# Queueing two weight splits behind the recombination, and the convolution behind them, in a decoder layer's up-projection

## The chip, the core and the metric

One core of a Trainium2 chip runs the whole program. The metric is the device time of one launch in microseconds (us): the median of 3 runs of the kernel before is 1353.44 us, lowest 1352.97, highest 1354.55.

## The reference

One decoder layer on 1024 positions of width 1024, all in float32: RMSNorm, two attention mixers side by side, a gated merge and a residual, then RMSNorm and a gated MLP, whose input side is the part that matters here:

```python
u = xn @ w_up                                # (1024,1024) @ (1024, 5632)
c = conv_b
for j in range(3):
    c = c + upad[:, j:j + S] * conv_w[j]     # causal, per channel
gate, val = jnp.split(c, 2, axis=-1)
x = x + (jax.nn.silu(gate) * val) @ w_down   # (1024,2816) @ (2816,1024)
```

## The kernel before, in words

**Arithmetic.** TensorE multiplies in a rounded 32-bit format. To keep float32 precision, every operand is split into a high part (a cast on ScalarE, ACT) and a low part, the source minus the high part (a subtraction on VectorE, DVE); a product is three matmuls: high·high, high·low, low·high.

**The up-projection** (`hidden`, lines 883 to 963) takes the 44 blocks of 128 output columns as 22 pairs j = 0..21: block j is the gate, block j + 22 the value. Each pair uses a seven-product scheme (Strassen-Winograd) instead of eight products. Its steps, with the names that the text uses:

- *Loading and sums* (`sum_pair`, L93 to L104). Two transfers from the SP queue bring the raw blocks: `raw` (L93, A11 and A12) and `rv` (L95, A21 and A22). GpSimd (POOL) makes the four sums in four operations of 128x512: L98 and L102 give S1 and S2, L103 and L104 give S3 and S4. The buffers of `rv` and of the sums are two deep, so the transfer of a later `rv` waits until the low part of A22 has been taken, and L103 waits until the low part of S3 and S4 of the pair before has been taken.
- *Splitting* (`split_pair`, L120 and L121): for each of (A11, A12), (S1, S2), (S3, S4) and (A22) a cast on ACT and a subtraction on DVE. The text calls the four DVE subtractions **low11** (`wl<-raw`, 128x1024), **low12** and **low34** (`sl<-sf`, 128x1024 each) and **low22** (`wl<-rv`, 128x512).
- *Products* P1, P2, P5, P6, P7, P3, P4 in this order, 12 matmuls of 128x128 by 128x512 each into a PSUM bank of its own (in the last pair P4 stands ahead of P3). P1 multiplies A11, P4 multiplies A22. In P4 the third matmul is the first that reads low22. A product may begin when the bank that it takes has been read: P5 of a pair takes the bank that L423 of the pair before reads.
- *Recombination* (`recombine`, L422 to L429): one copy on ACT and seven additions on DVE, 128x512, which read the banks and write the two halves `us`; L428 completes the first half, L429 (the block c21) the second.
- *Convolution and gate* (`conv`, `glu`). For each half: POOL scales by the norm factor (L1014), ACT starts the convolution (L1019), DVE adds two taps (L1020, L1021, both `c<-us,vecs,c`). Then ACT takes the SiLU (L1006), DVE multiplies gate and value (L1007), and SP stores the product (L1008). The text calls the DVE steps tap1 and tap2 of the first and second half.

While the products of pair j + 1 run on TensorE, the other engines recombine and convolve pair j, and prepare pairs j + 1 to j + 3. A scheduler sets the order of instructions on each engine by priorities; `issue_after` adds that everything issued under it stands behind the named instruction on its engine. The last pair has its convolution deferred into the down-projection, and in the last two rounds the hidden blocks 0 to 2 are split as well (L793).

Of the kernel before, what the change touches and what calls it, by code (L numbers as in the profile page):

```python
# [13 lines left out]
ALU = mybir.AluOpType  # L14
# [29 lines left out]
class Trunk:  # L44
    def __init__(self, tc, ins, out):
        self.tc, self.nc = tc, tc.nc
        (self.xT, self.w_in, self.w_br, self.w_mix, self.w_up, self.w_dn,
         self.vecs_d, self.bias_d) = ins
        self.out = out
        self.uid = 0  # L50
        self.stores = []
        self.uw = self.w22 = self.behind = None
        self.pin = False
        self.hs, self.defer, self.late = {}, [], []

    def name(self, s):
# [50 lines left out]
    def split_pair(self, g, v, sa, sb, skip=0, end=4):  # L107

        nc = self.nc
        ops = {}  # L110
        for pool, h, l, src, names in ((self.wp, "wh", "wl", g, ("A11", "A12")), (self.uw, "sh", "sl", sa, ("S1", "S2")),
                                       (self.uw, "sh", "sl", sb, ("S3", "S4")), (self.w22 or self.wp, "wh", "wl", v[:, 1:2], ("A22",)))[skip:end]:
            n = len(names)
            hi = self.tl(pool, [P, n, 4, P], h, F32R)
            lo = self.tl(pool, [P, n, 4, P], l, F32R)
            with ExitStack() as queue:
                if self.pin and ops:
                    for i in done:
                        queue.enter_context(self.tc.issue_after(i.ins))
                i = nc.scalar.copy(hi, src)  # L120
                j = nc.vector.tensor_tensor(lo, src, hi.bitcast(F32), ALU.subtract)  # L121
            if not ops:
                done = i, j
            for i, name in enumerate(names):
                ops[name] = hi[:, i], lo[:, i]
        self.pin = False
        return ops

    def load_raw(self, src, nk):
# [286 lines left out]
    def recombine(self, ps, us, tp, o):  # L416

        nc = self.nc
        c11, c12, c21, c22 = (us[w][:, o + hf * H2:o + (hf + 1) * H2] for w in range(2) for hf in range(2))
        s1, u3 = (self.tl(tp, [P, H2], n, bufs=1) for n in ("s1", "u3"))  # L420
        tt = nc.vector.tensor_tensor
        nc.scalar.copy(s1, ps["P1"])  # L422
        tt(c11, ps["P2"], s1, ALU.add)  # L423
        tt(s1, ps["P6"], s1, ALU.add)
        tt(u3, ps["P7"], s1, ALU.add)
        tt(c22, ps["P5"], u3, ALU.add)
        tt(s1, ps["P5"], s1, ALU.add)
        tt(c12, ps["P3"], s1, ALU.add)  # L428
        tt(c21, u3, ps["P4"], ALU.subtract)  # L429

    def keep(self, m, u, to):

# [450 lines left out]
    def hidden(self, pair):  # L883
        nc, tc = self.nc, self.tc
        with ExitStack() as ctx:
            e = ctx.enter_context
            psF = e(tc.tile_pool(name="psF", bufs=8, space=PSUM, reuse_waits="tile"))
            self.psT = psF
            xc2 = e(tc.tile_pool(name="xc2", bufs=1, side="right", reuse_waits="tile"))
            self.uw = e(tc.tile_pool(name="uw", bufs=3, side="right", reuse_waits="tile"))  # L890
            prods = (("P1", "A11", "B11"), ("P2", "A12", "B21"), ("P5", "S1", "T1"), ("P7", "S3", "T3"),
                     ("P3", "S4", "B22"), ("P6", "S2", "T2"), ("P4", "A22", "T4"))
            with tc.high_priority(400):
                w0 = self.split_pair(*pair)
            ready = {}
            for j in range(NF):
                w, ps = ready.pop(j) if j else (w0, {})
                if j == 0:

                    for name, a, b in prods[:5]:  # L900
                        ps[name] = self.tl(psF, [P, H2], "t")
                        self.product(ps[name], w[a], b, range(3), last=False)
                    for k in range(4):
                        hi, lo = self.split(*(xc2.tile([P, T], F32R, name=f"T42_{k}{p}") for p in "hl"), self.t42[k])
                        self.B["T4", k], self.B["T2", k] = ((hi[:, c], lo[:, c]) for c in (slice(0, H2), slice(H2, T)))
                        if k == HOLD:
                            self.behind, self.pin = self.lo, True
                    self.tctx.close()
                    tp = e(tc.tile_pool(name="tp", bufs=2, side="right", reuse_waits="tile"))
                    self.w22 = e(tc.tile_pool(name="w22", bufs=1, side="right", reuse_waits="tile"))  # L910
                    w22 = self.w22
                    ssq = self.tl(psF, [P, H2], "t")
                    for n, (name, a, b) in enumerate(prods[:5]):
                        self.product(ps[name], w[a], b, (3,), first=False)
                        if n == 4:
                            self.col_sums(ssq, [self.rstd], NB, 0)
                            with tc.high_priority(400):
                                rs = self.rstd_cols(ssq, 8, D)
                if j == NF - 1:

                    with tc.high_priority(50):
                        for k, r in enumerate(raw):
                            for hf in range(2):
                                h = self.tl(self.uw, [P, 2, H2], ("sh", "sl", "rv", "rv", "sh", "sl")[2 * k + hf], F32R, **({"bufs": 2} if k == 1 else {}))
                                self.hs[hf, k] = self.split(h[:, 0], h[:, 1], r[:, hf * H2:(hf + 1) * H2])
                        lo = self.lo
                for name, a, b in (prods[i] for i in ((0, 1, 2, 5, 3, 6, 4) if j == NF - 1 else (0, 1, 2, 5, 3, 4, 6) if j else range(7))):
                    if name not in ps:
                        ps[name] = self.tl(psF, [P, H2], "t")
                        self.product(ps[name], w[a], b, low_last=name == "P1")  # L930
                us = [self.tl(tp, [P, T + 2], "us", bufs=3) for _ in range(2)]
                if j == NF - 1:
                    self.defer.pop(0)(lo)
                    w22.tile([P, 104], F32, name="pad_w22")
                    self.xctx2.close()
                    self.uw = self.w22 = None
                    self.open_down()
                    self.deep = True
                    with tc.high_priority(100):
                        self.ahead(2)  # L940
                self.recombine(ps, us, tp, 2)
                if j < NF - 1:

                    w, ps = ready[j + 1] = self.next_w(), {}
                    if j == NF - 2:
                        raw = [self.tl(self.sfp[0], [P, T], "t42", bufs=1)] + [self.tl(self.sfp[0], [P, T], "sf") for _ in range(2)]
                        for k, r in enumerate(raw):
                            nc.sync.dma_start(r, self.hd[k])
                    for name, a, b in prods[:2 if j == 0 else 0]:
                        ps[name] = self.tl(psF, [P, H2], "t")  # L950
                        self.product(ps[name], w[a], b, low_last=name == "P1")
                if j == 0:
                    for hf in range(2):
                        sp = self.tl(psF, [P, H2], "t")
                        self.spread(sp, rs, hf * 4)
                        nc.scalar.copy(self.rstd[:, hf * H2:(hf + 1) * H2], sp)

                for w in range(2):
                    f = lambda after=None, j=j, w=w, us=us: self.glu(j, w, us[w], tp, after)
                    if j + w < NF - 1:  # L960
                        f()
                    else:
                        self.defer.append(f)

# [295 lines left out]
```

## Time and profile before

| | |
|---|---|
| median of 3 runs | 1353.44 us |
| profiled execution | 1352.23 us, of which the span on the core is 1350.4 us |
| granted clock of TensorE | 0.997 |
| busy: TensorE / DVE / ACT / POOL | 99% / 75% / 45% / 35% |
| pair 1's P1 begins / pair 21's P1 begins | 701.79 us / 1088.12 us |

In the timeline a row gives the start in us from the start of the span, the duration in us, the engine, the line, the operation, what it writes and reads, and in brackets the idle time ahead of it with what ended it. A matmul's duration is its way through the array; the next starts some 0.23 us after it, so the distance of starts tells the pace. DVE's rows overlap by about 0.08 us in the same way.

### The profile page before, as it was taken

Reading aid. Unit: us, or ns where it says so; the run is one execution under the profiler, and the core shown is the slowest. Engines: PE = TensorE matmul, PEld = TensorE weight load, DVE = VectorE, ACT = ScalarE, POOL = GpSimd, SP = SyncE. Lnnn points to the kernel's source line nnn. Section 1 sums busy time; section 2 is a strip of 40 time slices with the busy share of each in tenths; the row PEclk is TensorE's granted clock in tenths of the full one; section 3 lists DMA queues with packets and bytes.
Section 4 is the critical chain, followed back from the end, with each engine's and each line's share of the span. In section 5 each row is a group of like instructions: output and inputs, shape, how many; then the busy total and the mean of one; then the engine's idle time right before and its main releaser. Section 6 shows DMA issues by size and latency. Waiting matters only on the chain.

```text
span 1350.4 us, 17209 instructions
## 1 busy us (share of the span) xinstructions
PE 1332.3 (99%) x6304; PEld 1103.7 (82%) x6304; DVE 1009.0 (75%) x1457; ACT 603.3 (45%) x943; POOL 477.7 (35%) x349
## 2 busy tenths in 40 slices
PE   8999999999999999999999999999999999999997
PEld 6888888888887778888888888888888878888887
DVE  8847775288899876465679888888888988886454
ACT  8432232277667665334444334433443344333343
POOL 0436652010102124641455554555556520231011
PEclk9999999999999999999999999999999999999998
DMA  7423443966554236334422222222222239652342
GB/s 256 149 107 151 142 154 140 257 170 186 156 134 132 84 113 230 112 126 135 164 94 83 80 92 78 78 78 86 86 79 75 75 136 333 200 180 70 94 138 81
DMA packets 62468, 179.49 MB, mean 133 GB/s; under 512 B 6832, under 2 KB 15152, under 8 KB 62384
## 3 DMA queue, kind: packets, MB, share of 16 engines
q1 hardware_dynamic: 50928, 160.98, 36.8%
q10 hardware_dynamic: 11456, 17.41, 3.5%
q8 instruction: 50, 0.82, 0.3%
q14 instruction: 34, 0.28, 0.1%
HBM read 129.61 MB, written 48.76 MB: 132 GB/s over the span
## 4 chain that ended last, share of the span: by engine, by line
PE 64%; DVE 13%; issue 8%; POOL 7%; ACT 5%; DMA 2%; POOLq 0%; ACTq 0%; DVEq 0%; SPq 0%
PE t L879 6%; PE t L881 6%; PE t L880 6%; POOL us L1014 4%; PE y L1045 3%; PE d L1045 3%; PE g L176 3%; PE g L177 3%; PE g L178 3%; DVE wl L121 3%; PE sc L595 3%; PE sc L178 2%; PE sc L177 2%; PE sc L176 2%; PE d L1072 2%
## 5 line engine op out<-in xcount | busy, mean ns | idle before, releaser
L1019 ACT ACTIVATE c<-us,vecs 128x1024 f32<-128x1024 f32 x44 | 54.8, 1247 | 163.4 <-POOL us L1014 161.4
L1014 POOL TENSOR_TENSOR us<-us,rstd 128x1024 f32<-128x1024 f32 x42 | 100.3, 2405 | 52.0 <-DVE wl L143 34.6
L120 ACT CAST sh<-sf 128x1024 fp32r<-128x1024 f32 x62 | 65.0, 1050 | 113.8 <-POOL sf L102 68.6
L141 ACT CAST wh<-raw 128x1024 fp32r<-128x1024 f32 (+2 forms) x60 | 60.7, 1012 | 107.0 <-PE sc L177 30.5
L1020 DVE SCALAR_TENSOR_TENSOR c<-us,vecs,c 128x1024 f32<-128x1024 f32 x44 | 64.6, 1470 | 53.4 <-ACT c L1019 53.4
L143 DVE TENSOR_TENSOR wl<-raw,wh 128x1024 fp32r<-128x1024 f32 (+2 forms) x60 | 78.5, 1309 | 31.3 <-ACT wh L141 19.7
L98 POOL TENSOR_TENSOR sf<-rv 128x512 f32<-128x512 f32 x30 | 42.3, 1410 | 163.4 <-DVE sl L121 56.5
L121 DVE TENSOR_TENSOR sl<-sf,sh 128x1024 fp32r<-128x1024 f32 x62 | 86.1, 1391 | 11.5 <-ACT sh L120 11.4
L176 PE MATMUL g<-xh,wh 128*128 128x512 f32 x176 | 70.6, 401 | 0.1
L178 PE MATMUL g<-xh,wl 128*128 128x512 f32 x176 | 70.3, 400 | 0.0
L177 PE MATMUL g<-xl,wh 128*128 128x512 f32 x176 | 70.3, 399 | 0.0
L193 POOL TENSOR_TENSOR rs<-ms,mhalf 128x8 f32<-128x8 f32 (+2 forms) x9 | 14.5, 1606 | 157.3 <-DVE ms L191 146.7
L121 DVE TENSOR_TENSOR wl<-raw,wh 128x1024 fp32r<-128x1024 f32 (+1 forms) x35 | 61.2, 1748 | 3.7 <-ACT wh L120 3.6
L103 POOL TENSOR_TENSOR sf<-raw,rv 128x512 f32<-128x512 f32 x30 | 41.6, 1388 | 58.9 <-DVE sl L121 58.9
L599 DVE CUSTOM_DVE_ANT_0 L<-sc,bias 128x128 f32<-128x128 f32 (+7 forms) x64 | 47.7, 752 | 17.0 <-PE sc L595 13.8
L578 POOL MEMSET aT<- 128x128 f32 x32 | 6.1, 204 | 151.6 <-PE t L624 97.8
L102 POOL TENSOR_TENSOR sf<-sf,raw 128x512 f32<-128x512 f32 x31 | 58.5, 1886 | 1.6
L600 ACT ACTIVATE L<-L,sm 128x128 f32<-128x128 f32 (+7 forms) x64 | 49.6, 778 | 20.0 <-DVE sm L599 17.3
L1021 DVE SCALAR_TENSOR_TENSOR c<-us,vecs,c 128x1024 f32<-128x1024 f32 x44 | 57.2, 1302 | 0.6
L753 POOL TENSOR_TENSOR gr<-gr,rstd 128x1024 f32<-128x1024 f32 x16 | 40.4, 2531 | 40.0 <-DMA gr<-gd 39.9
L595 PE MATMUL sc<-u,u 128*128 128x512 f32 (+2 forms) x192 | 49.8, 358 | 0.0
L178 PE MATMUL sc<-mh,wl 128*128 128x512 f32 x126 | 49.1, 390 | 0.1
(479 smaller groups left out, 4323.9 us busy)
## 6 DMA issues: line engine op xcount, KB each, us to landing
u<-qd SPq DMA_DIRECT2D x72, 256.0 KB, 6.4
raw<-in_w_down SPq DMA_DIRECT2D x27, 512.0 KB, 3.7
raw<-in_w_in SPq DMA_DIRECT2D x25, 512.0 KB, 4.1
hr<-hd SPq DMA_DIRECT2D x50, 256.0 KB, 5.5
raw<-in_w_up SPq DMA_DIRECT2D x23, 512.0 KB, 3.5
hd<-c SPq DMA_DIRECT2D x22, 512.0 KB, 2.6
rv<-in_w_up SPq DMA_DIRECT2D x21, 512.0 KB, 3.5
gr<-gd SPq DMA_DIRECT2D x16, 512.0 KB, 3.6
```

The source lines that it names most:

```text
L120: i = nc.scalar.copy(hi, src)
L121: j = nc.vector.tensor_tensor(lo, src, hi.bitcast(F32), ALU.subtract)
L143: self.lo = (eng or nc.vector).tensor_tensor(wl, raw, wh.bitcast(F32), ALU.subtract)
L176: nc.tensor.matmul(ps, wh[:, kc + o, :], ah, start=first and n == 0, stop=False)
L177: nc.tensor.matmul(ps, wh[:, kc + o, :], al, start=False, stop=False)
L178: nc.tensor.matmul(ps, wl[:, kc + o, :], ah, start=False, stop=last and n == len(kcs) - 1)
L595: nc.tensor.matmul(sc[:, lo + n0:lo + n1], qs, k[c][part][:, n0:n1], start=part == 0, stop=part == 1)
L879: nc.tensor.matmul(ps, ah[:, k, :], bh, start=first and n == 0, stop=False, skip_group_check=skip)
L880: nc.tensor.matmul(ps, ah[:, k, :], bl, start=False, stop=False, skip_group_check=skip)
L881: nc.tensor.matmul(ps, al[:, k, :], bh, start=False, stop=last and n == len(ks) - 1, skip_group_check=skip)
L1014: i = (nc.vector if m % NF == 0 else nc.gpsimd).tensor_tensor(us[:, 2:], us[:, 2:], self.rstd, ALU.mult)
L1045: nc.tensor.matmul(ps, v[:, n, :], x, start=n == i == 0, stop=n == len(js) - 1 and i == 2)
```

## The change

In `hidden`, from pair 1 on, `next_w` (which splits the weights of pair j + 2) runs with `self.after` set to the last addition of the recombination (c21): the cast and the subtraction for A11 and A12 of pair j + 2 are issued after it. The cast and the subtraction of A22 of pair j + 1 and of A11, A12 of pair j + 2 are noted as `made`, and the convolutions of pair j are issued after these. Nothing is added to the work and nothing is taken from it.

```diff
@@ split_pair
+                if self.after is not None and names[0] == "A11":
+                    queue.enter_context(self.tc.issue_after(self.after.ins))
                 i = nc.scalar.copy(hi, src)
                 j = nc.vector.tensor_tensor(lo, src, hi.bitcast(F32), ALU.subtract)
             if not ops:
                 done = i, j
+            if names[0] in ("A11", "A22"):
+                ops["made", names[0]] = i, j
@@ recombine
-        tt(c21, u3, ps["P4"], ALU.subtract)
+        return tt(c21, u3, ps["P4"], ALU.subtract)
@@ hidden
-                self.recombine(ps, us, tp, 2)
+                c21 = self.recombine(ps, us, tp, 2)
+                made = []
                 if j < NF - 1:
+                    self.after = c21 if j else None
                     w, ps = ready[j + 1] = self.next_w(), {}
+                    self.after = None
+                    if j:
+                        made = [x[y] for x, y in ((w, ("made", "A22")), (self.wq[-1], ("made", "A11"))) if y in x]
@@ hidden, the convolutions
-                        f()
+                        with ExitStack() as queue:
+                            for i in made:
+                                for x in i:
+                                    queue.enter_context(tc.issue_after(x.ins))
+                            f()
```

The lines of the changed kernel stand 2 to 13 further down: the split is L122 and L123, the recombination L426 to L433, L1027, L1032, L1033, L1034 are the scaling and the three steps of the convolution, L1019 and L1020 SiLU and gate, L1021 the store.

The DVE queue in the steady part of the up-projection, before, from the last two additions of one pair (`us_1212`, `us_1213`) to the middle of the next pair's (`us_1237`); `wl_1202` is low22 of the pair after `us_1212`'s, `wl_1246` is low11:

```order
L428 TENSOR_TENSOR us_1212_7206<-t_1210_7180,s1_1214_7208 128x512
L121 TENSOR_TENSOR sl_1223_7233<-sf_1218_7222,sh_1222_7232 128x1024
L429 TENSOR_TENSOR us_1213_7207<-u3_1215_7209,t_1211_7193 128x512
L1020 SCALAR_TENSOR_TENSOR c_1228_7246<-us_1212_7206,vecs_80,c_1228_7246 128x1024
L121 TENSOR_TENSOR wl_1202_7097<-rv_1192_7076,wh_1201_7096 128x512
L1021 SCALAR_TENSOR_TENSOR c_1228_7246<-us_1212_7206,vecs_80,c_1228_7246 128x1024
L1020 SCALAR_TENSOR_TENSOR c_1229_7252<-us_1213_7207,vecs_80,c_1229_7252 128x1024
L1021 SCALAR_TENSOR_TENSOR c_1229_7252<-us_1213_7207,vecs_80,c_1229_7252 128x1024
L423 TENSOR_TENSOR us_1237_7350<-t_1231_7272,s1_1239_7352 128x512
L1007 TENSOR_TENSOR c_1228_7246<-c_1228_7246,c_1229_7252 128x1024
L121 TENSOR_TENSOR wl_1246_7373<-raw_1241_7362,wh_1245_7372 128x1024
L424 TENSOR_TENSOR s1_1239_7352<-t_1233_7298,s1_1239_7352 128x512
```

The same stretch of the DVE queue in the changed kernel, where `wl_1221` is the low11 that stood a round earlier before:

```order
L432 TENSOR_TENSOR us_1212_7206<-t_1210_7180,s1_1214_7208 128x512
L123 TENSOR_TENSOR sl_1223_7233<-sf_1218_7222,sh_1222_7232 128x1024
L433 TENSOR_TENSOR us_1213_7207<-u3_1215_7209,t_1211_7193 128x512
L123 TENSOR_TENSOR wl_1202_7097<-rv_1192_7076,wh_1201_7096 128x512
L123 TENSOR_TENSOR wl_1221_7229<-raw_1216_7218,wh_1220_7228 128x1024
L1033 SCALAR_TENSOR_TENSOR c_1228_7246<-us_1212_7206,vecs_80,c_1228_7246 128x1024
L1033 SCALAR_TENSOR_TENSOR c_1229_7252<-us_1213_7207,vecs_80,c_1229_7252 128x1024
L1034 SCALAR_TENSOR_TENSOR c_1228_7246<-us_1212_7206,vecs_80,c_1228_7246 128x1024
L1034 SCALAR_TENSOR_TENSOR c_1229_7252<-us_1213_7207,vecs_80,c_1229_7252 128x1024
L427 TENSOR_TENSOR us_1237_7350<-t_1231_7272,s1_1239_7352 128x512
L1020 TENSOR_TENSOR c_1228_7246<-c_1228_7246,c_1229_7252 128x1024
L428 TENSOR_TENSOR s1_1239_7352<-t_1233_7298,s1_1239_7352 128x512
```

Low22 and low11 now stand directly behind c21, ahead of every tap; tap1 of the second half stands ahead of tap2 of the first.

The ACT queue at the same place before (`wh` are the casts of the weights, `s1` is the copy of the recombination, the last `c<-c` is the SiLU):

```order
L120 CAST sh_1222_7232<-sf_1218_7222 128x1024
L1019 ACTIVATE c_1228_7246<-us_1212_7206,vecs_80 128x1024
L120 CAST wh_1201_7096<-rv_1192_7076 128x512
L1019 ACTIVATE c_1229_7252<-us_1213_7207,vecs_80 128x1024
L422 COPY s1_1239_7352<-t_1230_7259 128x512
L1006 ACTIVATE c_1228_7246<-c_1228_7246 128x1024
L120 CAST wh_1245_7372<-raw_1241_7362 128x1024
```

And in the changed kernel:

```order
L122 CAST sh_1222_7232<-sf_1218_7222 128x1024
L122 CAST wh_1201_7096<-rv_1192_7076 128x512
L1032 ACTIVATE c_1228_7246<-us_1212_7206,vecs_80 128x1024
L1032 ACTIVATE c_1229_7252<-us_1213_7207,vecs_80 128x1024
L426 COPY s1_1239_7352<-t_1230_7259 128x512
L122 CAST wh_1245_7372<-raw_1241_7362 128x1024
L1019 ACTIVATE c_1228_7246<-c_1228_7246 128x1024
```

The cast of A22 moves ahead of both convolutions, and the cast of A11 and A12 ahead of the SiLU. On SP the transfer of `rv` moves ahead of that of the later `raw`, and on POOL a memset moves behind L102; POOL's arithmetic keeps its order, and TensorE keeps its own.

More of the change, by code (lines that the diff above doesn't have):

```diff
@@ L52, in __init__ @@
         self.uw = self.w22 = self.behind = None
-        self.pin = False
+        self.pin, self.after = False, None
         self.hs, self.defer, self.late = {}, [], []
@@ L123, in split_pair @@
                 done = i, j
+            if names[0] in ("A11", "A22"):
+                ops["made", names[0]] = i, j
             for i, name in enumerate(names):
                 ops[name] = hi[:, i], lo[:, i]
-        self.pin = False
+        self.pin, self.after = False, None
         return ops
```

## The prediction

> **What bounds the kernel now.** The busy row of the page comes first: TensorE is busy all the time, so a change can only gain where TensorE waits, or lose by making it wait. The pace of the up-projection is then read from the starts of P1 in the timeline, of pairs 3, 4, 10 and 21.
>
> ```profile
> PE 1332.3 (99%) x6304; PEld 1103.7 (82%) x6304; DVE 1009.0 (75%) x1457; ACT 603.3 (45%) x943; POOL 477.7 (35%) x349
> ...
> 741.28 0.39 PE L873 MATMUL t<-B_0h,wh 128*128 128x512 f32 x1
> ...
> 760.32 0.39 PE L873 MATMUL t<-B_0h,wh 128*128 128x512 f32 x1
> ...
> 874.63 0.39 PE L873 MATMUL t<-B_0h,wh 128*128 128x512 f32 x1
> ...
> 1088.12 0.39 PE L873 MATMUL t<-B_0h,wh 128*128 128x512 f32 x1
> ```
>
> A pair takes 760.32 - 741.28 = 19.04 us, 0.2267 for each of its 84 matmuls; the later eleven take (1088.12 - 874.63) / 11 = 19.41. The 0.37 us that each loses sits in P4, as the waits of this stage and the matmuls around one low22 (then pair 21's) show:
>
> ```profile
> PEld t L881 <- DVE wl L121: 6.2, 13, 0.7
> ...
> 988.18 0.39 PE L880 MATMUL t<-T_0l,wh 128*128 128x512 f32 x1
> 988.64 0.50 PE L881 MATMUL t<-T_0h,wl 128*128 128x512 f32 x1
> 988.97 0.39 PE L879 MATMUL t<-T_1h,wh 128*128 128x512 f32 x1
> ...
> 1102.63 0.50 PE L881 MATMUL t<-T_0h,wl 128*128 128x512 f32 x1 [0.29 <-DVE wl L121]
> ```
>
> Thirteen times low22 is late. The eleven pairs lose 213.49 - 11 x 19.04 = 4.05 us, pair 21 another 0.6 at 1102.63 (0.46 late, and 0.11 behind it): about 4.7 us, all that the change can win here. Whether it wins them depends on why low22 is late, so DVE's round of pair 16 is read next, with POOL, ACT and SP.
>
> ```profile
> 981.87 1.22 DVE L121 TENSOR_TENSOR sl<-sf,sh 128x1024 fp32r<-128x1024 f32 x1
> 983.00 0.68 DVE L429 TENSOR_TENSOR us<-u,t 128x512 f32<-128x512 f32 x1
> 986.25 1.72 DVE L1020 SCALAR_TENSOR_TENSOR c<-us,vecs,c 128x1024 f32<-128x1024 f32 x1 [2.57 <-ACT c L1019]
> 987.90 0.68 DVE L121 TENSOR_TENSOR wl<-rv,wh 128x512 fp32r<-128x512 f32 x1
> 988.50 1.27 DVE L1021 SCALAR_TENSOR_TENSOR c<-us,vecs,c 128x1024 f32<-128x1024 f32 x1
> ...
> 992.21 0.68 DVE L423 TENSOR_TENSOR us<-t,s 128x512 f32<-128x512 f32 x1
> 992.81 1.72 DVE L1007 TENSOR_TENSOR c<-c,c 128x1024 f32<-128x1024 f32 x1
> 994.45 2.31 DVE L121 TENSOR_TENSOR wl<-raw,wh 128x1024 fp32r<-128x1024 f32 x1
> ...
> 997.28 1.21 DVE L121 TENSOR_TENSOR sl<-sf,sh 128x1024 fp32r<-128x1024 f32 x1
> ...
> 1001.13 1.22 DVE L121 TENSOR_TENSOR sl<-sf,sh 128x1024 fp32r<-128x1024 f32 x1
> ```
>
> ```profile
> 982.03 2.90 POOL L1014 TENSOR_TENSOR us<-us,rstd 128x1024 f32<-128x1024 f32 x1
> 984.90 2.00 POOL L1014 TENSOR_TENSOR us<-us,rstd 128x1024 f32<-128x1024 f32 x1
> 992.13 1.32 POOL L98 TENSOR_TENSOR sf<-rv 128x512 f32<-128x512 f32 x1 [5.23 <-DMA rv<-in_w_up]
> 993.52 2.16 POOL L102 TENSOR_TENSOR sf<-sf,raw 128x512 f32<-128x512 f32 x1
> ...
> 986.93 1.25 ACT L1019 ACTIVATE c<-us,vecs 128x1024 f32<-128x1024 f32 x1 [0.21 <-POOL us L1014]
> ...
> 988.61 0.33 SPq L95 DMA_DIRECT2D rv<-in_w_up  x1
> ```
>
> The round of low12 goes from 983.09 to 1002.35, 19.27 us: longer than the 19.04 of TensorE, which therefore falls into step. The obvious reading is that DVE's idle 2.57 us, while the scaling and ACT work, is room for low22 and low11. The durations say something else. Low11 takes 2.31 us beside L102; low12, of the same shape, takes 1.22. L1014 takes 2.90 where low12 is ahead of it and 2.00 behind another L1014. Earlier rows show how the two engines share:
>
> ```profile
> 724.79 1.72 DVE L1007 TENSOR_TENSOR c<-c,c 128x1024 f32<-128x1024 f32 x1
> ...
> 723.15 2.27 POOL L103 TENSOR_TENSOR sf<-raw,rv 128x512 f32<-128x512 f32 x1 [1.00 <-DVE sl L121]
> 725.38 2.28 POOL L104 TENSOR_TENSOR sf<-raw,sf 128x512 f32<-128x512 f32 x1
> ...
> 737.72 3.51 DVE L1021 SCALAR_TENSOR_TENSOR c<-us,vecs,c 128x1024 f32<-128x1024 f32 x2
> ...
> 737.86 2.29 POOL L98 TENSOR_TENSOR sf<-rv 128x512 f32<-128x512 f32 x1 [2.66 <-DMA rv<-in_w_up]
> ...
> 704.63 1.28 POOL L98 TENSOR_TENSOR sf<-rv 128x512 f32<-128x512 f32 x1
> 704.92 1.55 DVE L121 TENSOR_TENSOR wl<-rv,wh 128x512 fp32r<-128x512 f32 x1
> ```
>
> L103 ends at 725.42; L1007, waiting since 724.79, ends 1.09 later; L104, queued right behind L103, ends 1.15 after that. L98 gets in between two taps, and these take 3.51 instead of 2.5. So DVE operations with both inputs in SBUF and POOL's arithmetic take turns, and the one that has waited longer goes next. An addition that reads a PSUM bank is not held up (L423 beside L98: 0.68). The Trainium skill, "SBUF — State Buffer", section "Who interferes with whom", says the same: such a pair contends for a shared port, and the second to issue blocks fully until the first ends. The trace agrees, by the rows above; which of two waiting operations goes next the page leaves open, and the rows show it. By the page the moved low parts wait in the idle stretch too and the round stays near 19.5; read as free room, the stretch would give the whole 4.7 us.
>
> **The change, part by part.** The work stays, so what counts is how long the round becomes. Steps from one end to the next, all from the rows above: behind a POOL operation 1.08 for a DVE operation of 1024 and 0.56 for low22 (706.47 - 705.91); behind a DVE operation 1.86 for L1014 (984.93 - 983.09) and 1.15 for a sum; DVE behind DVE 1.13 for a subtraction or product, 1.20 for a tap, 0.60 for 512 elements.
>
> Tried on the round before, from low12's end: both L1014 3.81 (986.90), tap1 4.89, low22 5.49, the other three taps 9.09, L423 9.69 (measured 9.80). The transfer of `rv`, issued behind low22, lets L98 start 3.52 later (992.13) and end at 10.36; L1007 11.44, L102 12.59, low11 13.67, L424 14.27, low34 15.40, and 3.86 more to the next low12 (1002.35 - 998.49): 19.26, measured 19.27.
>
> The same steps in the new order: L1014 1.86; low22, waiting since c21, 2.42; second L1014 4.28; low11 5.36; tap1 6.56. `rv` is issued at 2.45, so L98 is ready near 6.0 and is next: 7.71. Tap1 of the second half 8.79, L102 9.94, tap2 11.02, tap2 12.22, L423 12.82, L1007 13.95, L424 14.55, low34 15.68, plus 3.86: **19.54**; I take 19.50, since overlaps shave a few hundredths. L98 and L102 now fall among the taps, where they cost DVE 1.15 each; before, L98 ran beside L423. That eats what the hidden waits gave.
>
> TensorE meets another wait first. Low22 is three us earlier in the round, but P5's bank is free only when L423 ends, at 12.82 instead of 9.80. P5 starts 36 matmuls (8.16 us) behind the start of the P4 before it, so P4 may start no sooner than 4.7 into the round; before, low22 asked for 5.1 (5.5 less two matmuls). The new wait of P1 for low11 asks for less: low11 ends at 5.36, and its first reader, eight matmuls into P1, stands 12 + 8 matmuls (4.5 us) behind P4's start, so 0.9 would do.
>
> The moves on the other queues stay covered. The cast of A22 stands ahead of both convolutions on ACT, behind the cast of S1 and S2, which L102 releases near 10; ACT is idle from then to the next L1014. SP now issues `raw` behind `rv`, some 3 us after it (low11's end), for a pair three rounds off. The taps stand behind low11 on DVE, and what waits for them, SiLU, product and store, ends at 13.95, long before the next round's convolutions take the two buffers.
>
> ```profile
> 743.99 1.21 DVE L121 TENSOR_TENSOR wl<-raw,wh 128x1024 fp32r<-128x1024 f32 x1
> ...
> 1091.51 0.95 DVE L143 TENSOR_TENSOR wl<-raw,wh 128x768 fp32r<-128x768 f32 x1
> ...
> 748.97 1.22 DVE L121 TENSOR_TENSOR sl<-sf,sh 128x1024 fp32r<-128x1024 f32 x1
> ...
> 1101.89 0.68 DVE L121 TENSOR_TENSOR wl<-rv,wh 128x512 fp32r<-128x512 f32 x1
> ```
>
> Start: low12 of pair 2's round ends at 750.19. The low11 at 743.99 leaves that round (1.13), but the one ahead of it now stands between the two L1014 and pushes L98: between 0 and 1.1 us earlier, I take 0.4, near 749.8. P4 of pair 3 starts 12 matmuls ahead of 760.32, at 757.60, 7.8 into the round: 3.1 us to spare, which 0.46 a pair uses up after seven pairs (before: 2.3 us, some 0.3 a pair). Seventeen rounds of 19.50 lead to 1081.3, the end of low12 in pair 19's. The round that follows has no L98 and L102 (2 x 1.03 less, since the tap behind takes 1.08 instead of 1.20), but a split (0.60) and L1007 (1.13) stand ahead of L423: it ends 12.5 in, and P5 of pair 21 starts at 1093.9; before, 1088.12 + 24 x 0.2267 = 1093.56. From L423 to low22 of pair 21 there are the low part of `w_down` (0.87, the row at 1091.51), L424 0.60, low34 1.13, the four additions to L428 2.73 (3.86 less low12), a split 0.60, L1014 1.86, a split 0.56, c21 and low22 1.20: 22.0 in, at 1103.3, against 1102.57. TensorE reads it 0.06 later, so the end moves by **+0.7 us**. With a rate uncertain by up to 0.08 a round (seventeen rounds: 1.4) and the start by 0.5, this is +0.7, from -1.2 to +2.6.
>
> Behind that the down-projection's waits hang on TensorE and on transfers issued in the same order, and move with it. The profiled execution (1352.23, span 1350.4) becomes 1352.9; it lies 1.2 under the median of the runs, to which I add the same: 1353.44 + 0.7 = **1354.1 us**.
>
> **Rivals.** *POOL keeps its turn through both L1014* (or there are no turns). No row shows a DVE operation waiting across two L1014. If it must, low22 ends at 4.37, low11 5.50, two taps 7.90; L98, ready at 7.92, goes behind the third (9.10) at 10.25; the fourth tap 11.33, L423 11.93 beside L102 (12.48), L1007 13.56, L424 14.16, low34 15.29: a round of 19.15, 0.11 over 19.04, which seventeen rounds (1.9 us) can't bring to the 4 us to spare. Without turns DVE's own steps (four taps 4.8, four operations of 1.13, low22 0.6, seven additions 4.5) are 14.4 a round, far under 19.04. Both give the whole 4.7: 1348.7 us. Against it: L1007 got in between L103 and L104.
>
> *The handing over costs more in the new order*, the rival on the other side. Its place is low22 between the two L1014, also shown by no row: L1014 behind it could take its full 2.00 instead of 1.86, and low22 its full 0.68 instead of 0.56. That is 0.26 a round, 17 x 0.26 = 4.4 us: 1358.5. It decides against the change from a round of 19.62 on (17 x 0.12 = 2.0 on top of 0.7, over 0.2%). Against it: each such step in the round before fits without it.
>
> *The queues don't do what the diff says*: the order rows show that they do.
>
> **How the numbers follow.** About 0.2% (2.7 us) is what a measurement of this kernel tells from no change. My forecast (near 19.5 a round; 1352.2 to 1356.0) has 0.68, the gain 0.16, the loss 0.16. The range, 1351.0 to 1357.6, takes in the forecast with its tails and most of the loss's span, and leaves the full gain out. The chances: faster 0.16, same 0.68, slower 0.16.
>
> **What would show it.** Low22 should end some 3 us earlier in the round and no longer hold P4 until pair 21; TensorE should instead wait in P5's first matmul for L427 (the old L423) from about pair 11 on, and its late pairs should take near 19.5 us. L98 and L102 should lie among the taps, each of them, and the tap behind, longer than alone. P1 should never wait for low11. If late pairs take 19.04 us, the turn-taking was read wrongly; if they take 19.7, the handing over was priced too low; a wait in the down-projection that isn't there now would break the sum elsewhere.

## The result, and the profile after

The changed kernel takes 1357.16 us (median of 11 runs, 1354.32 to 1360.02); the kernel before, run beside it, 1354.37 (11 runs). The ratio is 1.0022, with a 95% interval from 1.0013 to 1.0030: some 3.0 us slower, where 0.7 was forecast. The profiled execution of the changed kernel took 1358.04 us, its span is 1356.2.

First the place of the loss. The timeline of TensorE after: the P1 of pairs 1, 12 and 21, then the first matmul of the down-projection and TensorE's last ones; behind it the same first and last stations before.

```profile
704.32 0.39 PE L877 MATMUL t<-B_0h,wh 128*128 128x512 f32 x1
...
915.31 0.39 PE L877 MATMUL t<-B_0h,wh 128*128 128x512 f32 x1
...
1091.06 0.39 PE L877 MATMUL t<-B_0h,wh 128*128 128x512 f32 x1
...
1111.11 0.62 PE L1085 MATMUL d<-sh,wh 128*128 128x512 f32 x2
...
1349.95 0.38 PE L203 MATMUL y<-ident,rs 128*128 128x128 f32 x2
```

```profile
701.79 0.39 PE L873 MATMUL t<-B_0h,wh 128*128 128x512 f32 x1
...
1107.74 0.62 PE L1072 MATMUL d<-sh,wh 128*128 128x512 f32 x2
...
1344.18 0.63 PE L199 MATMUL y<-ident,rs 128*128 128x128 f32 x2
```

The nine late pairs take (1091.06 - 915.31) / 9 = 19.53 us each. From pair 1's P1 to the down-projection it takes 1111.11 - 704.32 = 406.79 us, before 405.95: **0.84 lost in the up-projection**. From there to the end of the last row it takes 1350.33 - 1111.11 = 239.22, before 1344.81 - 1107.74 = 237.07: **2.15 lost in the down-projection**, whose code the change doesn't touch. Together 2.99. The 2.5 us that lie ahead of 701.79 and 704.32 come from code that is the same in both, and go up and down from run to run: in two of the experiments below, which don't change that part either, the same P1 begins at 701.46 and 704.81. Another 0.3 lies behind TensorE's last row (5.87 us to the end of the span, before 5.59).

What TensorE's weight loads wait for after, from 880 to 1100 us (first row) and from 1100 to 1190 (the others), as total, times and longest; then the stretch from 1100 to 1190 before.

```profile
PEld t L883 <- DVE us L427: 5.9, 11, 0.6
...
PEld d L1085 <- DVE wl L147: 1.7, 1, 1.7
PEld t L885 <- DVE wl L123: 1.0, 1, 1.0
PEld y L879 <- DVE wl L147: 0.9, 1, 0.9
PEld d L1085 <- DVE sh L797: 0.6, 1, 0.6
PEld y L877 <- ACT wh L145: 0.5, 1, 0.5
```

```profile
PEld y L875 <- DVE wl L143: 0.8, 1, 0.8
```

The thirteen waits of P4 are gone but for pair 21's; eleven waits of P5's first matmul for L427 have taken their place. And the down-projection, which had one wait for `wl`, has three more: for `wl` (1.7), for `sh` (0.6) and for `wh` (0.5).

DVE's and POOL's round of pair 16 after, to be read against the stretch of before in the prediction:

```profile
985.12 1.22 DVE L123 TENSOR_TENSOR sl<-sf,sh 128x1024 fp32r<-128x1024 f32 x1
...
986.85 1.89 DVE L123 TENSOR_TENSOR wl<-rv,wh 128x512 fp32r<-128x512 f32 x1
988.67 3.02 DVE L123 TENSOR_TENSOR wl<-raw,wh 128x1024 fp32r<-128x1024 f32 x1
991.61 3.51 DVE L1033 SCALAR_TENSOR_TENSOR c<-us,vecs,c 128x1024 f32<-128x1024 f32 x2
995.04 3.50 DVE L1034 SCALAR_TENSOR_TENSOR c<-us,vecs,c 128x1024 f32<-128x1024 f32 x2
998.46 0.68 DVE L427 TENSOR_TENSOR us<-t,s 128x512 f32<-128x512 f32 x1
...
1004.64 1.22 DVE L123 TENSOR_TENSOR sl<-sf,sh 128x1024 fp32r<-128x1024 f32 x1
```

```profile
985.28 5.32 POOL L1027 TENSOR_TENSOR us<-us,rstd 128x1024 f32<-128x1024 f32 x2
992.36 1.67 POOL L98 TENSOR_TENSOR sf<-rv 128x512 f32<-128x512 f32 x1 [1.75 <-ACT s L426]
994.11 2.15 POOL L102 TENSOR_TENSOR sf<-sf,raw 128x512 f32<-128x512 f32 x1
```

DVE has no idle stretch over 0.11 us left, yet its round is 1004.64 - 985.12 = 19.52. Low22 takes 1.89 and low11 3.02 beside the two scalings, where they took 0.68 and 2.31; each couple of taps takes 3.5 with L98 and L102 among them. Counted from the end of low12 (986.34), low22 ends at 2.40, low11 at 5.35, the second tap1 at 8.78, the last tap at 12.20 and L427 at 12.80: within 0.02 of the steps that the prediction forecast.

### The profile page after: what moved, and what is told of

It reads as the page before. It is cut to its first block, busy times and chain, and to the rows that moved or that the text cites. A ratio compares the mean times of both kernels' runs of the same rounds, so it can differ in the third digit from the quotient of the medians.

```text
span 1356.2 us, 17171 instructions
## 1 busy us (share of the span) xinstructions
PE 1332.9 (98%) x6304; PEld 1102.7 (81%) x6304; DVE 1057.9 (78%) x1457; ACT 602.4 (44%) x943; POOL 493.5 (36%) x349
## 4 chain that ended last, share of the span: by engine, by line
PE 56%; DVE 23%; issue 11%; POOL 4%; DMA 4%; ACT 2%; SPq 0%; POOLq 0%; DVEq 0%; ACTq 0%
DVE c L1033 5%; PE t L885 4%; PE t L884 4%; PE t L883 4%; DVE wl L123 4%; PE y L1058 3%; PE d L1058 3%; PE sc L599 3%; PE g L180 3%; PE g L181 3%; PE g L182 3%; DVE c L1034 2%; DMA gr<-gd 2%; PE sc L182 2%; PE sc L181 2%
## 5 line engine op out<-in xcount | busy, mean ns | idle before, releaser
L1032 ACT ACTIVATE c<-us,vecs 128x1024 f32<-128x1024 f32 x44 | 54.8, 1248 | 168.5 <-POOL us L1027 167.2
L1027 POOL TENSOR_TENSOR us<-us,rstd 128x1024 f32<-128x1024 f32 x42 | 109.4, 2623 | 53.0 <-DVE wl L147 35.0
L147 DVE TENSOR_TENSOR wl<-raw,wh 128x1024 fp32r<-128x1024 f32 (+2 forms) x60 | 75.5, 1260 | 31.7 <-ACT wh L145 20.3
L123 DVE TENSOR_TENSOR sl<-sf,sh 128x1024 fp32r<-128x1024 f32 x62 | 86.3, 1395 | 11.5 <-ACT sh L122 11.5
L122 ACT CAST sh<-sf 128x1024 fp32r<-128x1024 f32 x62 | 63.0, 1045 | 59.5 <-PE t L884 43.3
L98 POOL TENSOR_TENSOR sf<-rv 128x512 f32<-128x512 f32 x30 | 48.2, 1608 | 99.5 <-DVE sl L123 56.5
L123 DVE TENSOR_TENSOR wl<-raw,wh 128x1024 fp32r<-128x1024 f32 (+1 forms) x35 | 76.0, 2171 | 3.7 <-ACT wh L122 3.6
L1033 DVE SCALAR_TENSOR_TENSOR c<-us,vecs,c 128x1024 f32<-128x1024 f32 x44 | 74.4, 1724 | 4.3 <-ACT c L1032 4.3
L1034 DVE SCALAR_TENSOR_TENSOR c<-us,vecs,c 128x1024 f32<-128x1024 f32 x44 | 73.2, 1696 | 0.0
L102 POOL TENSOR_TENSOR sf<-sf,raw 128x512 f32<-128x512 f32 x31 | 58.5, 1887 | 2.2
L1019 ACT ACTIVATE c<-c 128x1024 f32<-128x1024 f32 x22 | 23.4, 1064 | 77.9 <-DVE c L1034 77.9
L123 DVE TENSOR_TENSOR wl<-rv,wh 128x512 fp32r<-128x512 f32 x30 | 50.5, 1682 | 3.5 <-ACT wh L122 3.5
```

The costliest lines, as they stand in the source:

```text
L102: tt(sa[:, 1], sa[:, 0], g[:, 0], ALU.subtract)
L147: self.lo = (eng or nc.vector).tensor_tensor(wl, raw, wh.bitcast(F32), ALU.subtract)
L1027: i = (nc.vector if m % NF == 0 else nc.gpsimd).tensor_tensor(us[:, 2:], us[:, 2:], self.rstd, ALU.mult)
L1033: nc.vector.scalar_tensor_tensor(c, us[:, 1:T + 1], cw[1], c, ALU.mult, ALU.add)
L1034: nc.vector.scalar_tensor_tensor(c, us[:, 0:T], cw[0], c, ALU.mult, ALU.add)
```

## The experiments

**Which round makes the down-projection late?** Two kernels split the change: all rounds but the last one that has it, and that one alone.

```diff
-                    self.after = c21 if j else None
+                    self.after = c21 if 0 < j < NF - 2 else None     # not_last
+                    self.after = c21 if j == NF - 2 else None        # only_last
-                    if j:
+                    if 0 < j < NF - 2:                               # not_last
+                    if j == NF - 2:                                  # only_last
                         made = [...]
```

> The change in every round but the last one that has it (pair 20's): there the first tap of the convolution stands ahead of low22 again, as before the change, and nothing else differs from the changed kernel. Theory A, that the order of that last round makes the down-projection late (taps, SiLU and with them the cast and low part of w_down stand behind low22 on ACT and DVE): the two waits of the down-projection at 1113.00 (0.30 us) and 1162.45 (1.40 us) vanish, while low22 of pair 21 comes one tap later, so that its wait in P4 grows from 0.8 to about 2.2 us; near 1356.4 us, about 2 over before. Theory B, that the seventeen longer rounds before it make DVE late for the down-projection, whatever the last round's order: the two waits stay and the longer wait in P4 comes on top, 1358.5 us. In both the late rounds stay at 19.52.

> The change in pair 20's round alone: all rounds ahead of it as before, in the last one low22 stands ahead of the first tap. Theory A (the last round's order makes the down-projection late): the wait of P4 of pair 21 for low22 (0.46 us, and 0.11 behind it) goes, and waits of 1 to 2 us come in the down-projection; 1354.4 to 1355.8 us, the same as before or a little over. Theory B (the longer rounds do): no new wait in the down-projection, 0.6 under before, 1353.8 us.

Measured: not_last 1356.41 us (before, on this chip, 1354.11), ratio 1.0026 (1.0016 to 1.0036); only_last 1354.24, ratio 1.0001 (0.9992 to 1.0010). The waits of TensorE's weight loads, of not_last from 880 and from 1100 on:

```profile
PEld t L883 <- DVE us L427: 5.9, 11, 0.6
...
PEld t L883 <- ACT wh L122: 1.5, 1, 1.5
PEld t L885 <- DVE wl L123: 1.1, 1, 1.1
```

and of only_last from 1100 on:

```profile
PEld d L1085 <- DVE wl L147: 2.5, 2, 1.8
```

Theory A holds in both. With the old order in the last round, the three new waits of the down-projection are gone although the rounds ahead are as long as in the changed kernel; the price is in P4 of pair 21, which now waits for the cast of A22 (1.5) and for low22 (1.1). With the new order in the last round alone, P4 no longer waits and the down-projection does. From its first matmul to TensorE's last row the down-projection takes 236.84 us in not_last (1111.74 to 1348.58) and 239.14 in only_last (1108.73 to 1347.87). So the last round's order decides *where* TensorE pays for a late DVE. In the profile of only_last the up-projection wins 0.97 and what follows loses 2.07; the interval of its time is too wide to tell that 1.1 from nothing.

**By which way does it reach the down-projection?** ACT's and DVE's rows around the last convolution ahead of it, in the changed kernel (`wl` 128x768 is the low part of the third pieces of `w_down`):

```profile
1105.25 0.68 DVE L123 TENSOR_TENSOR wl<-rv,wh 128x512 fp32r<-128x512 f32 x1
...
1107.65 1.28 DVE L1034 SCALAR_TENSOR_TENSOR c<-us,vecs,c 128x1024 f32<-128x1024 f32 x1
...
1108.96 1.06 ACT L1019 ACTIVATE c<-c 128x1024 f32<-128x1024 f32 x1 [1.89 <-DVE c L1034]
1109.93 0.82 ACT L145 CAST wh<-raw 128x768 fp32r<-128x768 f32 x1
...
1110.78 0.96 DVE L147 TENSOR_TENSOR wl<-raw,wh 128x768 fp32r<-128x768 f32 x1 [1.26 <-ACT wh L145]
```

and in the kernel before:

```profile
1103.80 1.06 ACT L1006 ACTIVATE c<-c 128x1024 f32<-128x1024 f32 x1
1104.77 0.82 ACT L141 CAST wh<-raw 128x768 fp32r<-128x768 f32 x1
...
1105.62 0.96 DVE L143 TENSOR_TENSOR wl<-raw,wh 128x768 fp32r<-128x768 f32 x1 [0.65 <-ACT wh L141]
```

The cast stands behind the SiLU, the SiLU behind the second tap, the taps behind low22, and DVE's queue behind the cast. Before, the low part of `w_down` began 1107.74 - 1105.62 = 2.12 us ahead of the down-projection's first matmul; after, 1111.11 - 1110.78 = 0.33. The next kernel exchanges SiLU and cast on ACT and nothing else:

```diff
-        nc.scalar.activation(self.c0, self.c0, AF.Silu)
+        self.silu = nc.scalar.activation(self.c0, self.c0, AF.Silu)
...
                     with tc.high_priority(100):
                         self.ahead(2)
+                    tc.add_manual_dep(self.silu.ins, self.hi.ins.name, DependencyInfo(NoSync, DATA))
```

> The changed kernel with two instructions of ACT exchanged at the start of the down-projection: the cast of w_down's third pieces (L145, 1109.93 us in the profile after) stands ahead of the SiLU (1108.96) and no longer behind it. Theory A (the chain taps behind low22, SiLU, cast, low part L147, the splits behind it makes the down-projection late): the cast runs near 1107.1, L147 follows L427 at 1109.5 instead of 1110.8, all behind it comes 1.3 us earlier; the waits at 1113.00 and 1162.45 go or shrink to 0.1, near 1.6 under the changed kernel, 1355.5 us. Rival (the down-projection is late from its transfers, or from DVE's amount of work there): the waits stay, 1357.2 us.

Measured: 1355.03 us (before 1354.24), ratio 1.0008 (1.0000 to 1.0017). The rows of ACT and DVE, and the one matmul of the down-projection's first half (`d`) that still waits:

```profile
1106.57 0.84 ACT L145 CAST wh<-raw 128x768 fp32r<-128x768 f32 x1
1108.56 1.06 ACT L1020 ACTIVATE c<-c 128x1024 f32<-128x1024 f32 x1 [1.15 <-DVE c L1035]
...
1109.05 0.94 DVE L147 TENSOR_TENSOR wl<-raw,wh 128x768 fp32r<-128x768 f32 x1
...
1160.49 0.50 PE L1086 MATMUL d<-h,wl 128*128 128x512 f32 x1 [0.21 <-DVE wl L147]
```

L147 no longer idles for the cast, the wait for `sh` is gone, that for `wl` falls from 1.7 to 0.6 in the weight loads' view. The median lies 2.1 us under that of the changed kernel, with 1.6 forecast. In the profile the down-projection takes 237.75 us (1110.70 to 1348.45), 1.47 less than after and still 0.68 more than before; the up-projection keeps its loss (0.76). So the chain through SiLU and cast is shown for 1.47 of the 2.15; the rest goes with the last round's order too, as not_last shows, but its way was not followed.

**Is it the place of the sums that makes the round 19.5?** In late_sums, on top of not_last, L98 waits for the last tap of the round; late_all has the same wait on the changed kernel, whose last round it keeps; sums_only has it on the kernel before, there without the condition on `self.after`. Lines behind L98 stand two further down in the first two.

```diff
         i = tt(sa[:, 0], v[:, 0], v[:, 1], ALU.add)
+        if self.after is not None and self.tap2 is not None:
+            self.tc.add_manual_dep(i.ins, self.tap2.ins.name, DependencyInfo(Sync, DATA))
...
-        nc.vector.scalar_tensor_tensor(c, us[:, 0:T], cw[0], c, ALU.mult, ALU.add)
+        self.tap2 = nc.vector.scalar_tensor_tensor(c, us[:, 0:T], cw[0], c, ALU.mult, ALU.add)
```

> The kernel of the run not_last with one more wait: POOL's L98 starts only behind the fourth tap of the convolution, so that L98 and L102 lie beside the additions that read PSUM and beside the product instead of among the taps. All other queues keep their order. Theory A of the prediction (DVE operations with two SBUF inputs and POOL's arithmetic take turns, and L98 and L102 among the taps cost 1.15 us each): four taps end at 10.2 us after low12 instead of 12.2, the round needs about 18.7 and follows TensorE's 19.04, no wait is left in P5's first matmul or in P4 of the late pairs; about 4.4 us under before, 1350.0 us. Rival (the place of the sums is of no account; the moved low parts and the dependences among the DVE operations set 19.5): as not_last, 1356 us. Second rival (L102 and the cast behind it come too late for low12): the round becomes longer than 19.5 and the time 1360 us or more.

> The changed kernel, its last round too, with the wait that puts L98 behind the fourth tap. Taking turns gives rounds of 19.04 as in late_sums, and low22 of pair 21 comes early, so no wait in P4 at all: 4.7 us under before in the up-projection. If the last round's order makes the down-projection late, about 1 us of waits appears there and the time is near 1350.7 us; if only the longer rounds did, none appears and it is near 1349.7 us. If the place of the sums is of no account: as the changed kernel, 1357 us.

> The kernel before with the wait of late_sums alone: POOL's L98 behind the fourth tap, the low parts and the convolution in their old order. Taking turns: in the old order the taps end at 9.1 us after low12 and L98 starts at 9.05 already, beside L423, so nothing moves: 1354.1 us, within 0.2% of before. Rival (the wait on the sums brought all of late_sums' gain, the moved low parts none of it): 1348.8 us.

Measured: late_sums **1348.78 us** (before 1354.11), ratio 0.9964 (0.9953 to 0.9976); late_all 1349.79, ratio 0.9976 (0.9964 to 0.9989); sums_only 1357.54 (before 1354.24), ratio 1.0024 (1.0016 to 1.0033). DVE and POOL in late_sums, one round:

```profile
978.85 3.02 DVE L125 TENSOR_TENSOR wl<-raw,wh 128x1024 fp32r<-128x1024 f32 x1
981.79 2.47 DVE L1035 SCALAR_TENSOR_TENSOR c<-us,vecs,c 128x1024 f32<-128x1024 f32 x2
984.18 2.47 DVE L1036 SCALAR_TENSOR_TENSOR c<-us,vecs,c 128x1024 f32<-128x1024 f32 x2
986.57 0.68 DVE L429 TENSOR_TENSOR us<-t,s 128x512 f32<-128x512 f32 x1
...
997.53 3.02 DVE L125 TENSOR_TENSOR wl<-raw,wh 128x1024 fp32r<-128x1024 f32 x1
```

```profile
986.73 1.30 POOL L98 TENSOR_TENSOR sf<-rv 128x512 f32<-128x512 f32 x1 [1.06 <-DVE c L1036]
```

The taps are back at 2.47 a couple, L98 lies beside the addition L429, and DVE's round is 997.53 - 978.85 = 18.68, with 18.7 forecast. That is under TensorE's 19.04, so TensorE waits for nothing from 880 us to the end of the down-projection's first part (1190): the same view of waits is empty there. The up-projection takes 401.27 us (702.29 to 1103.56), 4.69 less than before, all that the prediction saw to be won there (4.7); another 1.14 comes from the down-projection. Late_all, with the last round's new order, waits there only once, as before; what I gave for the case that the order alone costs (1 us) did not come. DVE, 0.36 us a round faster than TensorE, has gained a lead: L149 begins at 1098.56, the down-projection at 1105.42, 6.9 us later, and so much covers the order. Between the two the intervals don't decide.

Sums_only is the miss: nothing was to move, and it is as slow as the changed kernel. DVE and POOL at the end of the taps, and what the weight loads wait for from 770 us on:

```profile
998.10 0.69 DVE L425 TENSOR_TENSOR us<-t,s 128x512 f32<-128x512 f32 x1
998.70 1.93 DVE L1009 TENSOR_TENSOR c<-c,c 128x1024 f32<-128x1024 f32 x1
...
998.26 1.29 POOL L98 TENSOR_TENSOR sf<-rv 128x512 f32<-128x512 f32 x1 [2.38 <-DVE c L1023]
```

```profile
PEld t L883 <- DVE wl L123: 10.3, 18, 0.8
```

Waiting for the tap, L98 begins 0.16 us behind the addition that follows the tap, and the product behind that addition takes 1.93. Before, L98's place varies: in pair 16's round, the one that the prediction steps through, it began 0.08 *ahead* of the addition (992.13 against 992.21) and the product took 1.72, but in the other steady rounds it began from 0.06 ahead to 0.32 behind, and the product took 1.86 on the average of the eleven late pairs. That is less than 0.1 us a round. The larger part was lost at the start, as DVE's low12 of an early round shows, then that of pair 2's round and, seventeen rounds later, of pair 19's (and this last one before):

```profile
732.74 1.35 DVE L123 TENSOR_TENSOR sl<-sf,sh 128x1024 fp32r<-128x1024 f32 x1 [2.92 <-ACT sh L122]
...
753.98 1.22 DVE L123 TENSOR_TENSOR sl<-sf,sh 128x1024 fp32r<-128x1024 f32 x1
...
1085.37 1.22 DVE L123 TENSOR_TENSOR sl<-sf,sh 128x1024 fp32r<-128x1024 f32 x1
```

```profile
1078.94 1.22 DVE L121 TENSOR_TENSOR sl<-sf,sh 128x1024 fp32r<-128x1024 f32 x1
```

An early L98 has to wait for pair 0's taps as well: it begins 22.04 us behind pair 1's P1 (726.85 - 704.81), before 9.40 (711.19 - 701.79). The cast of its sums is late, DVE idles 2.92 for it, and low12 of pair 2's round ends 50.39 behind that P1, before 48.40: 2.0 us lost. The seventeen rounds take 331.39 us, before 329.97: 1.4 lost, 0.08 in each. Together they are the 3.4 by which the up-projection is longer (409.35, from 704.81 to 1114.16, against 405.95). All these rounds are longer than TensorE's 19.04, so there are eighteen waits for low22 in place of thirteen. In late_sums the same wait delays the start too (low12 of pair 2's round ends 50.10 behind pair 1's P1), but its rounds of 18.68 make up for it. So the gain of late_sums needs both halves: the low parts in the idle stretch, and the sums out of the taps' way; each without the other was slower than before.

**Is low11 to blame?** The last kernel leaves low11 where it stood before the change.

```diff
-                    self.after = c21 if j else None
+                    self.after = None
...
-                        made = [... (w, ("made", "A22")), (self.wq[-1], ("made", "A11")) ...]
+                        made = [... (w, ("made", "A22")) ...]
```

> The changed kernel without the move of low11: low22 behind the recombination and the convolution behind it, low11 again behind the product, where it stood before. Taking turns, from the end of low12: low22 2.4, second scaling 4.3, taps 5.4 and 6.6, L98 7.7, tap 8.8, L102 9.9, tap 11.0, L427 11.6, product 12.8, low11 13.9, L428 14.5, low34 15.6, and 3.9 more: a round of 19.5 as in the changed kernel (low11 in the idle stretch wins as much as it loses by the sums), about 1356.5 us. If low11 in the idle stretch is what lengthens the round, rounds of 19.04 to 19.2 and 1350 to 1352 us.

Measured: 1358.00 us (before 1354.24), ratio 1.0029 (1.0020 to 1.0038). Low12 and the next low12 of DVE, and three rows of the weight loads' waits from 900 us on:

```profile
983.83 1.22 DVE L123 TENSOR_TENSOR sl<-sf,sh 128x1024 fp32r<-128x1024 f32 x1
...
1003.41 1.22 DVE L123 TENSOR_TENSOR sl<-sf,sh 128x1024 fp32r<-128x1024 f32 x1
```

```profile
PEld t L883 <- DVE us L427: 4.8, 9, 0.5
PEld t L883 <- DVE s L428: 2.7, 10, 0.3
PEld d L1085 <- DVE wl L147: 1.8, 1, 1.8
```

The round is 1003.41 - 983.83 = 19.58 (19.5 forecast), and 19.60 on the average of seventeen (low12 ends at 749.88 and 1083.02): low11 in the idle stretch is not what lengthens the round; it shortens it, by 0.08. With low11 back behind the product, the addition behind it (L428) comes later, and a second bank is waited for in ten pairs. The down-projection's waits stay.

## Where the prediction was right, and which step failed

- **The round.** Forecast 19.50 (19.54 by the sum), measured 19.52. The round of before that the prediction steps through (19.27) is one of the shortest: the seventeen average 19.41, from 19.27 to 19.64, because L98 begins now ahead of the addition and now behind it. After, all are between 19.51 and 19.53, so the change lengthens the round by 0.11 us, not by 0.25; the forecast of the end doesn't use that difference. The two engines take turns as read: late_sums moves nothing but L98 and L102 against not_last, and the round falls to 18.68, where the same steps gave 18.7. The rival with a gain (POOL keeps its turn, 19.15) is refuted by low22's 1.89 us between the two scalings; the one with a dearer handing over (19.62 or more) by the 19.52. The Trainium skill, "SBUF — State Buffer", section "Who interferes with whom", has the second operation blocked until the first ends; low22 (1.89, alone 0.68) and low11 (3.02) agree.
- **The new wait.** Forecast in P5's first matmul for L427, from about pair 11 on: eleven waits, one in each pair from 11 to 21. P1 never waits for low11.
- **The end of the up-projection.** Forecast +0.7 at low22 of pair 21, measured +0.84 at the first matmul of the down-projection. The stations on the way fit: low12 of pair 19's round ends 379.63 us behind pair 1's P1 (1083.95 - 704.32), with 379.5 forecast (1081.3 - 701.79). A start 0.3 earlier than forecast and seventeen rounds 0.02 longer nearly cancel there, which is luck.
- **What failed** is the step "behind that the down-projection's waits hang on TensorE and on transfers issued in the same order, and move with it". It was priced at nothing and cost 2.15 us. They hang on DVE and ACT as well: the taps, the SiLU, the cast and the low part of `w_down` stand in one chain behind low22 in pair 20's round, and its lead over TensorE was only 2.12 us. The new order took 1.8 of it: not_last gives back the waits, cast_first most of them, and only_last alone brings them. The prediction counted the taps' place behind low22 in the ordinary rounds, where the SiLU has a whole round of cover, and didn't look at the round that has none. Its own sign of a break elsewhere, a wait in the down-projection that wasn't there, is what came.
- **The size of the whole.** 0.84 and 2.15 make 2.99 us; the medians differ by 2.79, and the ratio gives 3.0. The time stays inside the range that was given, 0.4 us under its upper end, but above the forecast's own 1352.2 to 1356.0. The range reached so far up for a dearer handing over, which did not come; that the down-projection's 2.15 found room in it is luck. The chances did not foresee it either: the loss, 0.13 to 0.30% by its interval, lies around the 0.2% that the prediction took for the line to no change, and "slower" had 0.16.

Left open: the lead of `w_down`'s low part doesn't alone tell how long the down-projection waits. Only_last has 1.25 us of lead (1107.48 to 1108.73) and waits 2.5; cast_first has 1.65 (1109.05 to 1110.70) and waits 0.6. Sums_only, whose last round has the old order, has the whole 2.12 (1112.04 to 1114.16) and yet one weight load there waits 1.2 for the low part; its DVE idles 0.43 and 0.85 us for transfers of the hidden blocks (`hr`, at 1150.39 and 1151.93), where before it idled 0.33 once. These transfers, which lie between, were not tried by themselves.

## What to carry to other kernels

An idle stretch of one engine beside a busy one is room, in these runs, only for work that doesn't take turns with the busy one: before moving operations there, write the round as turns of both engines, and see what is pushed elsewhere. Here the low parts won nothing until the displaced sums were placed too, beside additions that read PSUM; then 0.36% was won. And read a change of a repeating order at its last repetition by itself: follow each moved instruction's queue on every engine until the next stage has its first operands.

## What the runs showed of the hardware

- A POOL operation that waited for the end of a DVE operation began 0.16 us behind the start of the DVE operation that follows it (986.73 against 986.57 in late_sums, 998.26 against 998.10 in sums_only).
- A difference of a few tenths in the round of an engine builds up unseen: DVE's rounds of 19.52 against TensorE's 19.04 made no wait until pair 11, and rounds of 18.68 brought DVE to a lead of about 7 us, which hid an order that costs 2 us without it.
- What lies ahead of pair 1's P1 is the same code in all nine kernels, and ended anywhere from 701.46 to 704.81 us in their profiles, so times inside a stage were compared from its own first matmul.
